# Row maximum on one core: three split rows, and 55 blocks through GpSimd in place of 38

## The chip, the cores and the metric

The kernel runs on 1 core of one Trainium2 chip. The metric is the device time of one execution in microseconds (us). The core's engines appear in the profile as PE (TensorE matmuls), PEld (its weight loads), DVE (VectorE), ACT (ScalarE), POOL (GpSimd) and SP (SyncE, which here only issues loads). Sixteen DMA engines move the data.

## What is computed

```python
def setup_inputs():
    batch, seq, dim = 32, 512, 1024
    return {"x": np.random.randn(batch, seq, dim).astype(np.float32)}

def reference(x):
    return np.max(x, axis=-1).astype(np.float32)
```

The input is 16,384 rows of 1,024 float32, 67.11 MB; the output is one float32 for each row.

## The kernel before

**Layout.** The rows are dealt to 128 partitions, so each partition gets 128 rows. From here on a "row" means one row in each partition: 128 x 1,024 float32, or 4 KB on each partition and 524,288 bytes in all. The work is 128 such rows. `BLOCKS` cuts them into loads: the first list is one contiguous block of the input of 112 rows in each partition, the second the last 16. Each number is one DMA of so many rows, called L0, L1 and so on, here L0 to L17. The last two rows are no loads: `PIECES` cuts each into two column pieces (604 + 420 and 568 + 456), each with its own DMA.

**Ring.** The loads go into one SBUF tile `ring` of `RING` = 47 rows, used again from the start once the end is reached. Its first 128 columns are `res`, where the maxima collect. `issue()` puts the loads into SP's queue in their order (line 209), each as soon as no step that still reads its part of the ring is left before it in the plan; the pieces follow (line 214). The loads' waits are on the readers of the ring's part, and on earlier loads.

**Plan.** `PLAN` is an order written out by hand for all compute engines. `in_turn` keeps each engine's instructions in that order. Its steps:

- `d<j>`: DVE takes the maximum along the columns of load j's rows, into `res` (line 74 by way of `maximum`). Rows that are shared (below) are left out.
- `SHARED = {j: (m, parts)}` says that of load j's last m rows the first `parts` blocks of 128 columns go through GpSimd. `p<j>` is DVE's maximum over the other columns of these rows, written to a small PSUM tile `got`. With `parts` = 8 there is nothing left and no `p`.
- `t<k>`: for one chunk of such blocks (at most 8 blocks) PE transposes each 128 x 128 block into PSUM (line 138), ACT copies the chunk to SBUF (line 144), and POOL takes the maximum over the partitions with a partition all-reduce (line 146).
- `b<k>`: PE brings each block's 128 maxima back to one column of `got` (line 156).
- `m<j>`: DVE takes the maximum over `got`'s partial results of load j, into `res`.
- `f<k>`: DVE takes the maximum of piece k. A row's first piece writes its maximum into the ring column just ahead of the second piece, and the second piece's instruction reads that column too.

The order of the tail before is

```python
... d16 m12 p17 t6 f0 b5 f1 f2 b6 m14 f3 m17
```

**Stores.** Both stores are issued by ACT, after all of ACT's copies. The first (the 112 columns of the first block, 56 KB, line 236) waits for `behind`, which is `f0`; the second (the last 16 columns, 8 KB, line 238) waits for the last maxima.

**Buffers.** The tiles of the GpSimd path rotate: two PSUM tiles for the transposes, two SBUF tiles for the copies, two for the all-reduce's results, and four small PSUM tiles `got`. PE has one order for transposes and returns, so a `b` that waits for POOL holds the transposes after it.

Of the kernel before, what the change touches and what calls it, by code (L numbers as in the profile page):

```python
# [10 lines left out]


BLOCKS = [
    [2, 13, 13, 15, 14, 11, 11, 10, 8, 8, 7],
    [4, 3, 2, 2, 1, 1, 1],
]
RING = 47  # L17


SHARED = {10: (3, 6), 12: (2, 6), 14: (1, 6), 17: (1, 2)}  # L20

PIECES = [(604, 420), (568, 456)]

PLAN = """
    d0 d1 d2 d3 d4 d5 d6 d7 d8 d9 t0 d10 t1 t2 p10 d11 b0 b1 t3 d12 t4 p12 d13 b2 m10 t5 d14
    p14 d15 b3 b4 d16 m12 p17 t6 f0 b5 f1 f2 b6 m14 f3 m17  # L30
""".split()

NOSYNC = mybir.DependencyInfo(mybir.DependencyClass.NoSync, mybir.DependencyReason.DATA)
# [4 lines left out]
def kernel(  # L38
# [53 lines left out]
    views = []  # L92
    last = len(PIECES)
    first = at = 0
# [13 lines left out]
    assert first == I  # L108
    shared = [SHARED.get(j, (0, C)) for j in range(len(loads))]

# [68 lines left out]
    room = I + at * D  # L179
    for q in range(len(PIECES[0])):  # L180
        for r, widths in enumerate(PIECES):
            c, w = sum(widths[:q]), widths[q]
# [85 lines left out]
```

## Time and profile before

| what | value |
|---|---|
| median of 4 runs | 163.61 us (163.54 to 163.71) |
| the profiled execution's own time | 163.55 us |
| its span | 161.8 us, of 306 instructions |
| DVE busy | 135.5 us (84%), 37 instructions |
| POOL busy | 16.2 us, 7 of its 11 instructions all-reduces |
| PE busy | 13.5 us, 76 matmuls |
| DMA | 67.18 MB, mean 415 GB/s over the span |

Between the span and the execution's time lie 1.75 us outside the profile's instructions. A busy time is an average over the span; the DVE, for example, is idle in the first quarter while the first loads arrive and has no gap of note at the end. So the order of the prediction's views goes from the whole to the last twenty microseconds.

### The profile page before, as it was taken

To read this page: it belongs to the slowest core of one execution; us is meant where nothing else is said; L and a number is where in the kernel's file an instruction comes from. 1 tells how busy PE (TensorE), PEld (TensorE's weight loads), DVE (VectorE), ACT (ScalarE), POOL (GpSimd) and SP (SyncE) were. 2 spreads that over 40 slices of the span, in tenths; PEclk is the share of its full clock that TensorE was granted. 3 is DMA by queue.
4 is the path that set the end of the run, shared out by engine and by line. 5 is a ranking of instruction groups with operands and counts; after the bars stand their busy time and mean duration, and the time that the engine had idled before them with its cause. 6 is when DMAs were issued, how large, how long until landed. Compare 5 with 4: busy or idle time off the path is not lost.

```text
span 161.8 us, 306 instructions
## 1 busy us (share of the span) xinstructions
PE 13.5 (8%) x76; PEld 11.7 (7%) x76; DVE 135.5 (84%) x37; ACT 6.5 (4%) x8; POOL 16.2 (10%) x11
## 2 busy tenths in 40 slices
PE   0000000000000000000000000000000000737662
PEld 0000000000000000000000000000000000727441
DVE  3500089969995499989999999999999999999994
ACT  3000000000000000000000000000000000231220
POOL 0000000000000000000000000000000000197991
PEclk9999999999999999999999999999999999995555
DMA  5999999995999978999898999799999999999991
GB/s 196 484 421 421 421 421 500 487 504 258 486 486 486 440 326 369 454 405 535 357 535 357 501 390 486 324 486 389 446 462 389 446 397 454 409 425 413 409 392 42
DMA packets 3456, 67.18 MB, mean 415 GB/s; under 512 B 640, under 2 KB 896, under 8 KB 1536
## 3 DMA queue, kind: packets, MB, share of 16 engines
q1 hardware_dynamic: 3168, 67.11, 97.0%
q10 hardware_dynamic: 288, 0.07, 0.2%
HBM read 67.11 MB, written 0.07 MB: 415 GB/s over the span
## 4 chain that ended last, share of the span: by engine, by line
DVE 49%; DMA 46%; another core or an unknown queue 3%; SPq 1%; issue 0%; DVEq 0%
DVE ring L74 47%; DMA ring<-in_x_dram 46%; DVE got L74 1%; SPq L209 1%; DVEq L263 0%
## 5 line engine op out<-in xcount | busy, mean ns | idle before, releaser
L74 DVE TENSOR_REDUCE ring<-ring 128x1 f32<-128x1024 f32 (+12 forms) x21 | 131.5, 6294 | 23.0 <-DMA ring<-in_x_dram 22.9
L146 POOL PARTITION_ALL_REDUCE top<-sb x7 | 16.0, 2353 | 142.0 <-ACT sb L144 142.0
L138 PE MATMUL ps<-ident,ring 128*128 128x128 f32 x38 | 8.8, 413 | 140.8 <-DMA ring<-in_x_dram 140.5
L138 PEld LDWEIGHTS ps<-ident,ring 128*128 128x128 f32 x38 | 7.4, 220 | 140.9 <-issue 140.9
L144 ACT COPY sb<-ps 128x768 f32<-128x768 f32 (+1 forms) x7 | 5.2, 739 | 150.0 <-PE ps L138 148.7
L156 PE MATMUL got<-ident,top 1*128 1x1 f32 x38 | 4.9, 237 | 4.6 <-POOL top L146 2.9
L156 PEld LDWEIGHTS got<-ident,top 1*128 1x128 f32 x38 | 4.3, 200 | 6.1 <-POOL top L146 5.4
L74 DVE TENSOR_REDUCE got<-ring 128x3 f32<-128x768 f32 (+3 forms) x4 | 3.0, 754 | 0.0
L144 ACT ACT_TABLE_LOAD x1 | 1.3, 1283 | 0.7 <-PEq L252 0.7
L79 DVE MEMSET ident<- 128x128 f32 x1 | 0.2, 165 | 0.8 <-PEq L252 0.8
L74 DVE TENSOR_REDUCE ring<-got 128x3 f32<-128x21 f32 (+3 forms) x4 | 0.6, 160 | 0.0
L86 DVE TENSOR_SCALAR rowno<-rowno 32x1 f32<-32x1 f32 x3 | 0.4, 146 | 0.1
L81 DVE TENSOR_TENSOR_SCAN colno<-ident 128x128 f32<-128x128 f32 x1 | 0.4, 424 | 0.0
L88 DVE TENSOR_SCALAR ident<-colno,rowno 128x128 f32<-128x128 f32 x1 | 0.3, 285 | 0.0
L83 DVE STREAM_TRANSPOSE rowno<-colno 128x32 f32<-128x32 f32 x1 | 0.2, 213 | 0.0
L252 POOL MEMSET const-float32-0.0<- 128x1 f32 x1 | 0.1, 99 | 0.2 <-issue 0.2
L252 POOL MEMSET const-bfloat16-1.0<- 128x1 bf16 x1 | 0.1, 102 | 0.0
L252 POOL MEMSET const-uint8-127<- 128x1 uint8 x1 | 0.1, 102 | 0.0
L252 POOL MEMSET const-float32-1.0<- 128x1 f32 x1 | 0.1, 99 | 0.0
L80 DVE MEMSET rowno<- 128x32 f32 x1 | 0.1, 85 | 0.0
## 6 DMA issues: line engine op xcount, KB each, us to landing
ring<-in_x_dram SPq DMA_DIRECT2D x2, 6656.0 KB, 27.5
ring<-in_x_dram SPq DMA_DIRECT2D x2, 5632.0 KB, 30.9
ring<-in_x_dram SPq DMA_DIRECT2D x2, 4096.0 KB, 32.3
ring<-in_x_dram SPq DMA_DIRECT2D x1, 7680.0 KB, 52.8
ring<-in_x_dram SPq DMA_DIRECT2D x1, 7168.0 KB, 36.8
ring<-in_x_dram SPq DMA_DIRECT2D x1, 5120.0 KB, 39.1
ring<-in_x_dram SPq DMA_DIRECT2D x1, 3584.0 KB, 39.4
ring<-in_x_dram SPq DMA_DIRECT2D x3, 1024.0 KB, 38.2
```

The costliest lines, as they stand in the source:

```text
L74: return in_turn("DVE", nc.vector.reduce_max(out=out, in_=in_, axis=X))
L79: in_turn("DVE", nc.vector.memset(ident, 1.0))
L81: in_turn("DVE", nc.vector.tensor_tensor_scan(out=colno, data0=ident, data1=ident, initial=-1.0, op0=ALU.add, op1=ALU.mult))
L83: in_turn("DVE", nc.vector.transpose(out=rowno, in_=colno[:, :32]))
L86: in_turn("DVE", nc.vector.tensor_scalar(out=part, in0=part, scalar1=float(q * 32), scalar2=None, op0=ALU.add))
L88: identity = in_turn("DVE", nc.vector.tensor_scalar(out=ident, in0=colno, scalar1=rowno[:, 0:1], scalar2=None, op0=ALU.is_equal))
L138: in_turn("PE", nc.tensor.transpose(out=ps[:, w:w + P], in_=rows(j)[:, loads[j][1] - m + r + i, c * P:(c + 1) * P], identity=ident,))
L144: in_turn("ACT", nc.scalar.copy(out=sb[:, :W], in_=ps[:, :W]))
L146: in_turn("POOL", nc.gpsimd.partition_all_reduce(top[:, :W], sb[:, :W], P, bass_isa.ReduceOp.max))
L156: in_turn("PE", nc.tensor.transpose(out=share(j)[:, c, r + i:r + i + 1], in_=tops[k][0:1, w:w + P], identity=ident[0:1, 0:1],))
L209: load = nc.sync.dma_start(out=rows(issued), in_=src)
L252: nc = _bacc.Bacc("TRN2", target_bir_lowering=False, num_devices=1)
```

## The change

The loads become fewer and larger at the start (up to 16 rows), three rows in place of two are cut in two pieces, with the first pieces of the three rows loaded one after the other and then the second pieces, and eight loads in place of four give blocks to GpSimd: 55 blocks in ten chunks in place of 38 in seven. The first of them comes early (one row of L3, two blocks). The DVE gets 7 partials in place of 4 and 8 merges in place of 4. Loads and pieces together are 22 DMAs in both.

```diff
 BLOCKS = [
-    [2, 13, 13, 15, 14, 11, 11, 10, 8, 8, 7],
-    [4, 3, 2, 2, 1, 1, 1],
+    [2, 13, 16, 16, 15, 13, 12, 10, 9, 6],
+    [4, 3, 2, 2, 1, 1],
 ]
 RING = 47
-SHARED = {10: (3, 6), 12: (2, 6), 14: (1, 6), 17: (1, 2)}
+SHARED = {3: (1, 2), 7: (1, 3), 8: (2, 8), 9: (6, 2), 10: (4, 2), 11: (1, 6), 13: (2, 2), 15: (1, 4)}
-PIECES = [(604, 420), (568, 456)]
+PIECES = [(488, 536), (560, 464), (624, 400)]
 PLAN = """
-    d0 d1 d2 d3 d4 d5 d6 d7 d8 d9 t0 d10 t1 t2 p10 d11 b0 b1 t3 d12 t4 p12 d13 b2 m10 t5 d14
-    p14 d15 b3 b4 d16 m12 p17 t6 f0 b5 f1 f2 b6 m14 f3 m17
+    d0 d1 d2 d3 t0 p3 b0 m3 d4 d5 d6 t1 d7 p7 t2 d8 t3 b1 b2 t4 m7 p9 t5 b3 t6 m8 p10 b4 b5
+    d11 t7 p11 m9 d12 b6 m10 p13 t8 b7 d14 t9 m11 p15 f0 b8 f1 m13 f2 f3 f4 b9 f5 m15
 """.split()
```

## The prediction

> **What bounds the kernel now.** I read the page first, then the table of windows, the waits of SP's queue, the timeline of the tail, and the groups by shape.
>
> ```profile
> span 161.8 us, 306 instructions
> ...
> PE 13.5 (8%) x76; PEld 11.7 (7%) x76; DVE 135.5 (84%) x37; ACT 6.5 (4%) x8; POOL 16.2 (10%) x11
> ...
> q1 hardware_dynamic: 3168, 67.11, 97.0%
> ```
>
> The DVE is the busiest engine, yet the load queue q1 occupies the DMA engines for 97.0% of the span. The windows say where (columns: span, length, PE, PEld, DVE, ACT and POOL busy, PE clock, DMA share, GB/s):
>
> ```profile
> 71.80:110.60 38.80, 0.00 (x0) 0.00 (x0) 38.67 (x3) 0.00 (x0) 0.00 (x0) 1.00 0.99 427
> 154.00:155.00 1.00, 0.57 (x6) 0.49 (x6) 1.00 (x2) 0.67 (x1) 1.00 (x2) 0.50 1.04 418
> 156.50:157.00 0.50, 0.22 (x2) 0.00 (x0) 0.50 (x2) 0.18 (x1) 0.50 (x1) 0.50 1.04 376
> 158.20:158.40 0.20, 0.01 (x1) 0.00 (x0) 0.20 (x2) 0.00 (x0) 0.20 (x1) 0.50 0.00 0
> 158.40:158.60 0.20, 0.14 (x2) 0.14 (x2) 0.20 (x1) 0.00 (x0) 0.01 (x1) 0.50 0.11 31
> 158.60:158.80 0.20, 0.20 (x2) 0.15 (x2) 0.20 (x3) 0.00 (x0) 0.00 (x0) 0.50 0.84 235
> 158.80:159.00 0.20, 0.03 (x1) 0.00 (x0) 0.20 (x3) 0.00 (x0) 0.00 (x0) 0.50 0.09 20
> ```
>
> The DMA share stays near 1 until the last piece, so no ring wait starves the queue; the little traffic from 158.4 on is the first store, alone. Both DMA and DVE are full from 71.8 on.
>
> ```profile
> SPq L214 <- DMA ring<-in_x_dram: 18.2, 4, 8.1
> ```
>
> Each of the four pieces was issued when the load eight places ahead landed: L10 to L13 at 138.56, 143.47, 147.16, 149.64 (112, 116, 119, 121 rows). Issue plus time to landing gives the others: L2 36.74 (28 rows), L4 71.86 (57), L5 85.12 (68), L7 110.61 (89), L9 130.05 (105), and the last piece 149.64 + 9.0 = **158.64**. L2 to L10 is 84 rows and 8 DMAs in 101.82 us: with 0.05 for a DMA, **1.2075 us a row**. The last 16 rows and 11 DMAs took 20.08 us, which leaves **0.07 for a small DMA**.
>
> ```profile
> 71.86 71.22 DVE L74 TENSOR_REDUCE ring<-ring 128x14 f32<-128x14336 f32 x7 [0.78 <-DMA ring<-in_x_dram]
> ...
> 157.67 0.38 ACTq L236 DMA_DIRECT2D out_dram<-ring  x1
> ...
> 158.80 0.62 DVE L74 TENSOR_REDUCE ring<-ring 128x1 f32<-128x457 f32 x1
> 159.33 0.15 DVE L74 TENSOR_REDUCE ring<-got 128x1 f32<-128x3 f32 x1
> 159.52 0.34 ACTq L238 DMA_DIRECT2D out_dram<-ring  x1
> ```
>
> The last reduction starts 0.16 after its piece lands, held by f2 and m14; m17 ends at **159.48** and the last store follows. So the end is set by two chains that are level: the last landing plus one small reduction, and the DVE's backlog.
>
> ```profile
> L74 DVE TENSOR_REDUCE ring<-ring 128x8 f32<-128x8192 f32 x2 | 17.4, 8683 | 0.0
> L74 DVE TENSOR_REDUCE ring<-ring 128x1 f32<-128x1024 f32 x4 | 4.8, 1211 | 0.0
> ...
> L74 DVE TENSOR_REDUCE ring<-got 128x1 f32<-128x7 f32 x1 | 0.2, 155 | 0.0
> ```
>
> From 8 rows (8.683) and one (1.211) a DVE row costs 1.0674 us and an instruction 0.14 on top; each starts 0.08 before the one ahead ends (d10 at 138.67, d9 ended 138.75), so 0.06 net for a reduction and 0.075 for a merge. Test on before: from d7's start, 110.64, 49 rows less 38 blocks (4.75 rows) are 44.25 rows, 47.23 us; 18 reductions 1.08, 4 merges 0.30, the last overlap 0.08: 159.33. Measured 159.48: **0.15 of small waits** to carry over.
>
> **The change part by part.**
>
> *Loads.* Both versions have 128 rows and 22 DMAs, so by the row law the last landing stays at 158.64 if the queue is never empty. Ring waits: L4 waits for d1 (35.07, as before), L5 for d2 (57.6), L6 for d3, p3 and t0 (76.8), L7 for d4 (94.0), L8 and L9 for d5 (108), the rest for d6 (121) or for the load eight places ahead. At each of these at least one load of 12 rows or more (14 us) is still to land. On SP, whatever waits holds what is behind it, and there are always those 14 us. Cost 0; were that cover gone, a stall would go straight to the end.
>
> *Pieces.* One row more goes in pieces, one one-row load and one large load fewer. At equal DMA count that is 0. By the windows, pieces move at 376 GB/s and one-row loads at 418: 1.394 against 1.254 us a row, +0.14. The row law meets the four pieces' own landings (156.76, 157.57, 158.06, 158.64) within 0.1, so I take 0.05, nearer to 0. A rule speaks against this part. "DMA: Bandwidth & Descriptors" (the Trainium skill, section on the anatomy of one DMA) fits 2.0 us plus bytes over 436 GB/s to each GpSimd-issued DMA; by that, six pieces against four would be an estimated 4 us more if each were paid in turn. The row above it says otherwise for queued ones: the 228 KB piece landed 0.58 us after the 210 KB one.
>
> *The DVE's backlog.* L6 of after is 87 rows in 7 DMAs: 110.61 - 2 x 1.2075 - 0.05 = 108.14. d4 starts at L4's landing (62 rows: 77.9), ends 94.0, d5 at 107.9, so the DVE waits 0.2 for L6. The early p3, t0, b0 and m3 (0.94 + 0.15 on the DVE) lie before L4's landing (d3 from 59.7 to 75.9) and cost nothing; without that gap 1.1. From 108.17: 53 rows less 53 blocks (6.625) are 46.375 rows, 49.50 us; 18 reductions 1.08; 7 merges 0.53; overlap 0.08: 159.36, with the 0.15 of waits **159.51**. Seventeen blocks taken from the DVE are 2.27 us, but 15 of them only pay for the later start: fewer rows are done by L6 (87, where L7 had 89) and three merges and two partials more lie in the tail. The backlog stays level.
>
> *GpSimd's path.* 768 columns take 2.5 to 2.58 us and 256 took 1.1 (3.63 for the last two), so 1,024 take 3.27, 512 take 1.82. Two transposes took 0.66 and six 1.51, eight are 1.94; copies 0.80 and 0.37, so 1.01; six returns 0.80, so eight 1.02. L8 (106 rows) lands at 131.2: t2 and t3 hold POOL from 134.3 to 140.9; L9 at 138.5: t4 from 141.6, t5, then t6 to 150.0; b6 ends 151.1, and the DVE wants m10 at 108.17 + 40.375 rows and 12 instructions = 152.0. t9: L15 lands at 154.60; transposes 1.09, copy 0.59, all-reduce 1.82, returns 0.59 and 0.25 of handoffs end at 158.95, with m15 wanted at 159.3. Hidden, by 0.9 and 0.4 us. A 1,024-wide one is not in the trace: from 2.6 (the 768 row) to 4.4 (four times the 256 row); 3.27 lies on the line through both rows.
>
> *The first store.* It waits for f0 (ends 156.2) and is behind ACT's t9 copy (156.4); before it was issued at 157.67, 0.8 before its traffic, which then met no load. Now that traffic falls at 157.2 to 157.6, among the last pieces. Price: 0.2 x (0.11 + 0.84 + 0.09) = 0.21 us of all 16 engines; bounds 0 and 0.21 on the last landing. As the share there is 1.03 and nothing is free, I take 0.21. The same page's section on issuing engines says that DMAs from different engines share the 16 and interleave; by it 0.21, were queues separate 0.
>
> *Sum.* Last landing 158.64 + 0.05 + 0.21 = 158.90; f5 (401 columns, 0.56) starts at 158.93, m15 0.08 before its end, 0.15 long: **159.56**. The backlog says 159.51. The later is 0.08 after 159.48; the profiled execution of 163.55 becomes 163.63, and as the median of the runs is 0.06 above it, **163.7**. The two small pieces' gain (f3's 0.62 is now 0.56, 0.1 less waiting) is eaten by the store.
>
> **The rivals.**
>
> *GpSimd late (slower).* POOL has 0.73 us idle between t3 and t4, then t4, t5, t6 run on end. If an 8-block all-reduce takes x longer than 3.27, b6 is 4x - 0.73 later; it decides from x = 0.41 (0.9 of slack). At 0.65 more (a fifth) m10 is 1.0 late and all the DVE's tail with it: 164.7. For: no 1,024-wide row. Against: 768 ran at 2.5 to 2.58 every time, DVE busy or not.
>
> *Landing sooner (faster).* Without the collision the end is 0.26 sooner by landing, but the backlog holds 159.51: no gain. Over 0.33 needs the loads faster too, say 0.05 less for each of seven large DMAs, which moves L6 and the end by 0.35: 163.3. Against: 13 rows took 15.70 and 15 rows 18.14, both 1.21 a row.
>
> *The 16-row loads aren't single runs (slower).* They put 65,536 bytes on a partition; the longest in the trace is 61,440. Cut into 4 KB runs, 32 rows at 1.254 in place of 1.2075 lose 1.5 us: 165.2. Nothing in the trace hints at it.
>
> **How the numbers follow.** No change that can be told, as summed: 0.74, its own range 163.4 to 164.0. GpSimd late 0.12, landing sooner 0.08, runs cut 0.04, the rest 0.02. A measurement of this kernel tells about 0.2% (0.33 us) from no change. Of the forecast's 0.74, some 0.08 lies above that (piece bound of 0.14, the 0.15 of waits doubled, m15 late) and 0.01 below. Faster 0.09, same 0.65, slower 0.26. The range reaches to 164.4, into the late GpSimd, and down to 163.35.
>
> **What would show it.** Right: last piece landing at 158.6 to 159.0, the first store at about 156.4, no DVE wait after 108.2 over 0.3, L6 at 108.1, all-reduces of 1,024 at 3.3, 3,168 packets on q1. Wrong: a DVE wait on a return, PE's or POOL's; DMA share under 0.95 in a window between 40 and 157 us; a landing 0.4 or more from 158.9.

## The result and the profile after

The changed kernel takes **163.73 us** (median of 53 runs, 163.52 to 165.51), the kernel before 163.62 us (73 runs, 163.51 to 164.07). Their ratio is 1.003, with a 95% interval of 1.0019 to 1.0041. Median and ratio differ because the 53 times lie in two groups: 37 from 163.52 to 164.08 (median 163.66) and 16 from 164.93 to 165.51 (median 165.18). Nothing lies between, and no time of the kernel before lies in the upper group. So seven executions in ten are level with before, as forecast, and three in ten take some 1.5 us more. I call the second kind "late"; what makes them late is the subject of the experiments. Their spans, from 163.1 to 163.7 us against 161.7 to 162.2, hold all of it.

The profiled execution is one of the level ones, 163.56 us. Its page (row 5 has busy time, mean ns and idle time before):

```profile
span 161.8 us, 399 instructions
PE 20.6 (13%) x110; PEld 17.2 (11%) x110; DVE 133.6 (83%) x41; ACT 8.6 (5%) x11; POOL 23.4 (14%) x14
...
q1 hardware_dynamic: 3168, 67.11, 96.9%
q10 hardware_dynamic: 288, 0.07, 0.2%
q8 instruction: 1, 0.02, 0.0%
...
L146 POOL PARTITION_ALL_REDUCE top<-sb x10 | 23.2, 2356 | 134.9 <-ACT sb L144 134.9
```

The span is that of before to 0.1 us. The DVE has 1.9 us less to do and POOL 7.2 us more, off the path. One line is new: queue q8, of the kind that the profile calls instruction, moved one packet of 16,384 bytes. I read it as a fetch of a part of an engine's program (e2 shows that it is PE's); PE's instructions rose from 76 to 110 pairs of a weight load and a matmul.

The timeline of the tail, beside the lines shown of before:

```profile
77.35 0.16 DVE L74 TENSOR_REDUCE ring<-got 128x1 f32<-128x3 f32 x1 [0.53 <-PE got L156]
...
108.22 22.61 DVE L74 TENSOR_REDUCE ring<-ring 128x12 f32<-128x12288 f32 x2 [0.19 <-DMA ring<-in_x_dram]
...
156.28 0.38 ACTq L236 DMA_DIRECT2D out_dram<-ring  x1
...
156.95 2.49 DVE L74 TENSOR_REDUCE ring<-ring 128x1 f32<-128x624 f32 x4
...
159.36 0.15 DVE L74 TENSOR_REDUCE ring<-got 128x1 f32<-128x5 f32 x1
...
159.54 0.34 ACTq L238 DMA_DIRECT2D out_dram<-ring  x1
```

L6's reduction starts at 108.22 after a wait of 0.19. From there the DVE waits neither for a load nor for a return: m15 ends at 159.51, against m17's 159.48. The one wait on a return is m3's, at 77.35, for b0; the DVE waits 0.45 us more for L4 right after it, so it costs nothing. The DMA view of this tail (KB, us from issue to landing) has the second thing that is new:

```profile
out_dram<-ring ACTq DMA_DIRECT2D x1, 56.0 KB, 4.0
out_dram<-ring ACTq DMA_DIRECT2D x1, 8.0 KB, 1.4
```

The first store needed 4.0 us to land, where it had needed 1.6. It was issued at 156.28, but its first packet went at 157.88, when the loads were nearly drained (their last packet ends at 158.24). 135 of its packets have gone by 158.5. The other nine, the share of one of 16 DMA engines (144 / 16), go from 159.17 to 159.58. The trace does not name a packet's engine, but the fetch runs from 158.11 to 159.19, so I read it as one engine held by the fetch. As the last store is issued only at 159.54, this delay costs nothing here.

### The profile page after: what moved, and what is told of

Same layout as the page of the kernel before. It is cut to its first block, busy times and chain, and to the rows that moved or that the text cites. A ratio compares the mean times of both kernels' runs of the same rounds, so it can differ in the third digit from the quotient of the medians.

```text
span 161.8 us, 399 instructions
## 1 busy us (share of the span) xinstructions
PE 20.6 (13%) x110; PEld 17.2 (11%) x110; DVE 133.6 (83%) x41; ACT 8.6 (5%) x11; POOL 23.4 (14%) x14
## 2 busy tenths in 40 slices
DMA packets 3457, 67.19 MB, mean 415 GB/s; under 512 B 640, under 2 KB 1024, under 8 KB 1664
## 3 DMA queue, kind: packets, MB, share of 16 engines
q1 hardware_dynamic: 3168, 67.11, 96.9%
## 4 chain that ended last, share of the span: by engine, by line
DVE 47%; DMA 44%; issue 5%; another core or an unknown queue 1%; SPq 0%; DVEq 0%
DMA ring<-in_x_dram 44%; DVE ring L74 41%; DVE got L74 7%; SPq L209 0%; DVEq L263 0%
## 5 line engine op out<-in xcount | busy, mean ns | idle before, releaser
L74 DVE TENSOR_REDUCE ring<-ring 128x2 f32<-128x2048 f32 (+13 forms) x18 | 119.5, 6666 | 24.4 <-DMA ring<-in_x_dram 24.4
L146 POOL PARTITION_ALL_REDUCE top<-sb x10 | 23.2, 2356 | 134.9 <-ACT sb L144 134.9
L138 PE MATMUL ps<-ident,ring 128*128 128x128 f32 x55 | 13.7, 426 | 116.1 <-DMA ring<-in_x_dram 106.1
L138 PEld LDWEIGHTS ps<-ident,ring 128*128 128x128 f32 x55 | 10.6, 223 | 116.7 <-issue 115.8
L144 ACT COPY sb<-ps 128x1024 f32<-128x1024 f32 (+4 forms) x10 | 7.4, 747 | 147.2 <-PE ps L138 147.2
L74 DVE TENSOR_REDUCE got<-ring 128x1 f32<-128x768 f32 (+6 forms) x7 | 12.9, 1845 | 0.0
L156 PE MATMUL got<-ident,top 1*128 1x1 f32 x55 | 7.4, 244 | 22.4 <-DVE got L74 16.4
L156 PEld LDWEIGHTS got<-ident,top 1*128 1x128 f32 x55 | 6.6, 212 | 25.1 <-issue 17.8
L74 DVE TENSOR_REDUCE ring<-got 128x1 f32<-128x3 f32 (+7 forms) x8 | 1.3, 157 | 0.5 <-PE got L156 0.5
```

The costliest lines, as they stand in the source:

```text
L74: return in_turn("DVE", nc.vector.reduce_max(out=out, in_=in_, axis=X))
L138: in_turn("PE", nc.tensor.transpose(out=ps[:, w:w + P], in_=rows(j)[:, loads[j][1] - m + r + i, c * P:(c + 1) * P], identity=ident,))
L144: in_turn("ACT", nc.scalar.copy(out=sb[:, :W], in_=ps[:, :W]))
L146: in_turn("POOL", nc.gpsimd.partition_all_reduce(top[:, :W], sb[:, :W], P, bass_isa.ReduceOp.max))
L156: in_turn("PE", nc.tensor.transpose(out=share(j)[:, c, r + i:r + i + 1], in_=tops[k][0:1, w:w + P], identity=ident[0:1, 0:1],))
```

## The experiments

Late executions here are those above 164.5 us. "PE" is the number of PE's instructions that the trace records, waits included; a transpose is two of them. Nearly all late executions have spans of 162.9 us or more. Two have not, counted in brackets: one of e1 (164.95) and one of e11 (164.89) have spans of 162.1 and 162.0, like the level ones beside them, and what they take longer lies outside the profile's instructions. Whatever delayed these two did not delay the last store.

| kernel | PE | q8 packet in the profile, us | late | median us (before beside it) | ratio, 95% interval |
|---|---|---|---|---|---|
| before | 167 | none | 0 of 73 | 163.62 | |
| after | 242 | 158.11 | 16 of 53 | 163.73 (163.62) | 1.0019 to 1.0041 |
| e1, 50 blocks | 218 | 158.36 | 2 of 12 (+1) | 163.86 (163.64) | 1.001 to 1.0053 |
| e2, before + 40 | 247 | 158.02 | 1 of 11 | 163.69 (163.64) | 0.9993 to 1.0027 |
| e3, after + 12 | 266 | 158.13 | 6 of 12 | 164.20 (163.64) | 1.0013 to 1.0059 |
| e4, store late | 242 | 158.39 | 3 of 12 | 163.75 (163.64) | 1.0004 to 1.0051 |
| e5, fewer returns | 168 | none | 0 of 11 | 164.08 (163.84) | 1.0004 to 1.0022 |
| e9, after + 80 | 402 | 142.34 | 5 of 5 | 165.07 (163.83) | 1.0068 to 1.0094 |
| e10, before + 12 | 191 | none | 0 of 11 | 163.78 (163.83) | 0.9993 to 1.001 |
| e11, before + 24 | 215 | none | 0 of 12 (+1) | 164.00 (163.83) | 1.0006 to 1.0024 |

The kernel before was some 0.2 us slower beside e5 to e11 than beside e1 to e4, so each is read against the before of its own row.

**e1: the two early shares left out.**

```diff
-SHARED = {3: (1, 2), 7: (1, 3), 8: (2, 8), 9: (6, 2), 10: (4, 2), 11: (1, 6), 13: (2, 2), 15: (1, 4)}
+SHARED = {8: (2, 8), 9: (6, 2), 10: (4, 2), 11: (1, 6), 13: (2, 2), 15: (1, 4)}
-    d0 d1 d2 d3 t0 p3 b0 m3 d4 d5 d6 t1 d7 p7 t2 d8 ...
+    d0 d1 d2 d3 d4 d5 d6 d7 t0 d8 ...
```

> The changed kernel without the shares of L3 and L7: 50 blocks in place of 55, 20 PE instructions and their waits fewer (222 recorded or less in place of 242), two partials and two merges fewer on the DVE. Of 53 executions of the changed kernel 37 took 163.5 to 164.1 us and 16 took 164.9 to 165.5. Theory A, a fetch of instructions: its trace has one packet of 16 KB on the instruction queue q8, at 158.2 to 159.2, which the kernel before has not; PE's longer program calls for it, and where it gets in ahead of the last loads' packets the end is 1.4 us later. Then here q8 is gone and no execution lies above 164.5; the times are 163.6 to 164.0, as the DVE has 0.25 us more to do after L6. Theory B, the earlier first store among the pieces: the store still falls at 156.3, so about three in ten stay near 165.2. Theory C, the 65,536-byte runs of L2 and L3: they are still there, so three in ten stay near 165.2.

Nine times lie at 163.71 to 164.01 (median 163.84) and three at 164.95 to 165.55. The packet is still there, at 158.36: 218 instructions are still too many. The step meant to remove the fetch did not remove it, so this run decides nothing between the theories. The level times are some 0.2 us above the changed kernel's 163.66, about what was expected of the DVE, but half of that lies outside the span (1.91 us between span and time, 1.80 in the changed kernel).

**e2: the kernel before with a longer PE program.**

```diff
+    ps = psum.tile([P, D], F32)
+    for _ in range(40):
+        in_turn("PE", nc.tensor.transpose(out=ps[:, :P], in_=ident, identity=ident))
```

> The kernel before with 40 transposes of the identity more at its start (between 2.5 and 12 us, PE has nothing else to do there; their result is not used): 80 PE instructions more, 247 recorded in place of 167. Loads, stores, DVE and GpSimd work are those of before. Theory A: one 16 KB packet on q8 near the end, and a part of the executions, a tenth to all, at 164.8 to 165.6 us. Theories B and C: 163.6 us throughout, as before.

The packet appears, at 158.02, in a kernel whose loads, stores and plan are those of before. One of eleven executions is late, at 165.33, with a span of 163.5. That PE's longer program calls the fetch is shown; that it makes executions late is only hinted at by one of eleven.

**e3: the changed kernel with 12 such transposes (the same edit in after, `range(12)`).**

> The changed kernel with 12 transposes of the identity at its start: 24 PE instructions more, so that the instruction at which the fetch is asked for is reached some 3 to 4 us sooner, with loads still queued. Theory A: the 16 KB packet falls at about 154 to 156, always ahead of the last pieces, and all or nearly all executions are at 164.3 to 165.5. Theories B and C: as the changed kernel, seven in ten at 163.7, three in ten at 165.2.

Six of twelve are at 164.72 to 165.16, the others at 163.55 to 163.68. More are late, but not nearly all; and in the profile, a level one, the packet still lies at 158.13. The fetch had not moved ahead of the last pieces, so theory A in this form misses.

**e4: the first store held until f4.**

```diff
-            if behind is None:
+            if k == 4:
                 behind = inst
```

> The changed kernel with its first store held until f4 (158.9) in place of f0. Theory B: no execution above 164.5. Theories A and C: three in ten stay near 165.2 us. Beside that, by the prediction's term for the store, the last landing comes up to 0.21 us sooner and the executions not delayed take 163.55 in place of 163.65.

Three of twelve stay late (165.03 to 165.40), so the early store is not the cause. The other nine have a median of 163.71, not the 163.55 that the prediction's store term asks for, against 163.66 of the changed kernel: holding the store back gains nothing. By the prediction's sums it could gain little in any case, as the DVE's backlog holds the end at 159.51.

**e5: one return for each row of a chunk, in place of one for each block.** The kernel leaves out the other blocks' maxima, so its output is not the rows' maximum, and its merges read fewer values; the rest is kept.

```diff
 def back(k):
...
-            for c in range(parts):
+            for c in range(1):
...
 def merge(j):
...
+        some = share(j)[:, 0:parts + 1:parts, :] if parts < C else share(j)[:, 0:1, :]
```

> The changed kernel with one return of a block for each row of a chunk in place of one for each block (18 returns in place of 55); the other blocks' results are left out, and a merge reads only what was written. 74 PE instructions fewer: 168 recorded, about the 167 of the kernel before. Loads with their 65,536-byte runs, the early first store, POOL's and ACT's work, the DVE's partials and every wait of a merge on a return stay. Theory A (a longer PE program brings a 16 KB instruction fetch, which in some executions delays the last loads): no packet on q8, no execution above 164.5, the times at 163.55 to 163.95. If the long runs of L2 and L3, the store or the all-reduces were behind the late executions: three in ten near 165.2 us.

Eleven times, all between 163.99 and 164.16, beside a before of 163.75 to 164.01. All lie above the 163.55 to 163.95 that I expected. The spans do not (161.9 to 162.1, as before's); the extra lies outside them, 2.06 us in place of before's 1.78, and is not explained. The DMA view has no q8 any more:

```profile
DMA packets 3456, 67.18 MB, mean 415 GB/s; under 512 B 640, under 2 KB 1024, under 8 KB 1664
...
q1 hardware_dynamic: 3168, 67.11, 96.9%
q10 hardware_dynamic: 288, 0.07, 0.2%
```

The 65,536-byte loads, the early store, the ten all-reduces and the order of the merges are all still there. Were three in ten late as in the changed kernel, none of eleven would have a chance of 0.7 to the 11th, 2%. Taking PE instructions away took the fetch and the late executions away together.

**e6 to e8: profiles of three single executions.** e6 and e7 run e3's kernel, e8 the changed one.

> The changed kernel with 12 transposes of the identity at its start once more, for one profile. Half of its executions took 164.7 to 165.2. In one of these, theory A: the 16 KB packet starts before 157, with loads still queued, the last landing is 1 to 1.4 us later than 158.7 and f5 waits for it. Rival A2: the fetch falls after the loads as before, and PE waits for its instructions: b9 comes late and m15 waits for it, with the landings unchanged. In the other half: the packet at 158.1 to 158.4.

> The same kernel, one more profile, with the same two readings: an execution above 164.5 us shows a 16 KB packet before 157 and late landings (A), or unchanged landings and a late b9 (A2).

> The changed kernel itself, one more profile, with the same two readings: above 164.5 us the 16 KB packet lies before 157 and the landings behind it are late (A), or the landings are unchanged and b9 is late (A2); at 163.5 to 164.1 us the packet lies at 158.1 to 158.4.

e6 caught a late execution: 164.94 us. e7 (163.83) and e8 (163.72) are level, with the packet at 158.19 and 158.24, as expected of a level one. For the late one both readings that I had written down are wrong. e6's tail in the timeline:

```profile
159.07 0.56 DVE L74 TENSOR_REDUCE ring<-ring 128x1 f32<-128x401 f32 x1
159.55 0.15 DVE L74 TENSOR_REDUCE ring<-got 128x1 f32<-128x5 f32 x1
159.73 0.34 ACTq L242 DMA_DIRECT2D out_dram<-ring  x1
```

Loads, PE and DVE end on time: m15 at 159.70, the last store issued at 159.73. What is late comes after that. The same execution's DMA view from 159.5 to 163 us, then SP's waits:

```profile
q10 hardware_dynamic: 144, 0.01, 2.7%
q8 instruction: 1, 0.02, 1.7%
issues: line engine op xcount, KB each, median us to landing
out_dram<-ring ACTq DMA_DIRECT2D x1, 8.0 KB, 2.6
```

```profile
SPq L267 <- DMA out_dram<-ring: 4.3, 2, 3.0
```

and the same two lines in e7:

```profile
out_dram<-ring ACTq DMA_DIRECT2D x1, 8.0 KB, 1.4
...
SPq L267 <- DMA out_dram<-ring: 3.1, 2, 2.5
```

The fetch runs here from 160.32 to 161.29, and the last store lands 2.6 us after its issue in place of 1.4. 135 of its 144 packets start from 160.57 on within 0.3 us; the last nine, again one engine's share, start from 161.28 on, as the fetch ends. SP's wait for the stores, 3.1 us in e7, is 4.3 here: **the 1.2 us by which the execution is late**. Its span is 163.2, e7's 162.0. Half of the 1.2 us is the late packets themselves: the last one ends at 161.35, in e7 at 160.75. The other half lies between the last packet and the landing, 0.98 us in place of 0.36, and what fills it the trace does not show. Reading A2, that the end waits for PE's instructions, does not fit: PE's last matmuls are done by 159.3, before the fetch starts, and PE's next recorded instruction comes 0.30 us after the store's landing in e6 as in e7.

So, by this reading, the fetch holds one of 16 DMA engines for 1 us. At 158.1 it meets the first store, which has time; at 160.3 it meets the last store, for which the end waits.

**e9: the changed kernel with 80 transposes more.**

> The changed kernel with 80 transposes of the identity at its start (160 PE instructions more, 402 recorded). Theory A3, after the look at a late execution: the 16 KB instruction fetch holds up the packets of a store on its one DMA engine; at 158.2 it meets the first store and costs nothing, at 160.4 it meets the last store, whose nine packets on that engine then come 1 us late and move the end by 1.2 to 1.5. If the place in PE's program where the fetch is asked for sets its time, it is asked for here some 20 us sooner, is served at the latest when the loads end at 158.2, and no execution lies above 164.5 us: 163.55 to 163.85 throughout. If the fetch's time does not depend on PE's place, or more than one fetch comes, three to five in ten stay near 165.

All five times are 165.06 to 165.27, the opposite of what I expected. The fetch did move with PE's place in its program, to 142.34, but it didn't wait for the loads' end. The DVE's timeline:

```profile
144.98 3.36 DVE L74 TENSOR_REDUCE got<-ring 128x4 f32<-128x3072 f32 x1 [0.69 <-DMA ring<-in_x_dram]
148.67 2.29 DVE L74 TENSOR_REDUCE ring<-ring 128x2 f32<-128x2048 f32 x1 [0.33 <-DMA ring<-in_x_dram]
...
160.85 0.15 DVE L74 TENSOR_REDUCE ring<-got 128x1 f32<-128x5 f32 x1
```

L10 lands at 144.97 where it landed at 143.46 in after; p10 waits 0.69 us and d11 0.33, and m15 starts 1.49 us later than after's 159.36. Some 0.2 us of both was there before the fetch (L9 landed at 138.76, in after at 138.57), so the fetch's part is 1.3. This is theory A as first stated: among the loads, the fetch delays one engine's share of all that follows, and the end with it. The last load packets show it too: from 158.64 they start one at a time, mostly some 0.07 us apart, until 159.75, as one engine's would that is a microsecond behind the others. So the fetch cost 1.2 to 1.3 us in the two places where a profile shows its cost, over the last store (e6) and among the loads (e9), and nothing between the last load and the last store.

**e10 and e11: where the fetch begins (e2's edit with `range(12)` and `range(24)`).**

> The kernel before with 12 transposes of the identity at its start: 191 PE instructions recorded, between 168 (no fetch) and 218 (a fetch). One or the other: no packet on q8 and all times at 163.5 to 163.95, or one packet and about a tenth to three tenths of the executions near 165.2.

> The kernel before with 24 such transposes: 215 PE instructions recorded. By A3 one packet of 16 KB on q8, as at 218, and some executions near 165.2 us; without a packet, none above 164.5.

Neither profile has the packet, at 191 and 215 recorded instructions; e1 has it at 218. I had expected it at 215. e10 is level throughout (one time, 164.11, is above the range given). e11 has one time of 164.89 beside eleven of 163.86 to 164.06. Its span of 162.0 is theirs, so it is not late in the way of e6 or e9. The eleven lie 0.15 us above before, outside the span, like e5's, and this is open too.

## Why the prediction was right or wrong

The number and the range held: 163.7 was forecast for 163.73, in 163.35 to 164.4, and the likeliest case, that the two level chains stay level, is what 37 of 53 executions show. By the median the change is +0.07%, inside the 0.2% that I called no change; by the ratio, +0.3%, it is slower, because the mean carries the late executions. That part was forecast by no case. The close hit of 163.7 is partly luck: the level executions have a median of 163.66, and the late ones lift it to 163.73.

- **Row law and ring waits.** L4 landed at 77.9, L6 at 108.2, L8 at 131.3 (77.9, 108.1, 131.2 forecast); 3,168 packets. The DMA share was 0.95 to 1.06 in the stages from 36.7 to 158.1 us, so no ring wait starved the queue (windows of 4 us between 40 and 64 us scatter in both kernels, from 0.71 to 1.13 in before and from 0.72 to 1.21 in after, so a low one is no sign of a stall). The 16-row loads ran at the row law, so that rival is out.
- **DVE's backlog.** It began at 108.22 and reached m10 at 152.06 (152.0 forecast) and m15's end at 159.51 (159.51 by the backlog). Right to the size of its parts. As the DVE never waited after 108.22, it was this chain that set the end, and not the last landing, which the sum had put later (159.56).
- **GpSimd's times.** The 1,024-wide all-reduce took 3.26 us (3.27), the 512-wide 1.78 (1.82); b9 ended at 159.09 and m15 started at 159.36. Hidden, so the rival of a late GpSimd is out.
- **Pieces.** From L8's landing to the last one, 22 rows and 13 DMAs took 158.80 - 131.26 = 27.54 us; the row law gives 22 x 1.2075 + 13 x 0.07 = 27.48. The term of 0.05 stands at 0.06.
- **The first store, a mis-sized term.** It was priced at 0.21 us on the last landing, with its traffic 0.8 after the issue. Its packets came from 1.60 after the issue on, when all but 50 of the 3,168 load packets had started, and the row law leaves 0.01 for it. The term measured about 0. e4, without the store there, is no faster, but could have shown little of it. The last landing came at 158.80 in place of 158.90, and 0.07 of its difference from before's 158.64 was there at the first load already (the DVE's first reduction started at 5.37, not 5.30). The forecast of 0.08 over before was right partly by luck: this term stood where other small differences were.
- **The step that failed: GpSimd's path costed by its engines' time alone.** Each added block is a transpose and a return, four PE instructions; 17 blocks are 68. They were priced at nothing because PE is idle, and in time that is right. What they bring is a 16 KB fetch, which no row of before could show because it didn't happen there, and with it, as e5 and e6 indicate, the 16 of 53 executions that take 1.5 us more. "Runtime: NRT & Kernel Launch" of the Trainium skill (section on instruction fetch mechanics) says that a program is fetched in 16 KiB blocks of 256 instructions, and that the cost of crossing from one to the next is mostly hidden. The size is that of the packet; hidden it was, if all late executions are the fetch's, in 37 of 53.

What stays open is why the same program's fetch falls at 158.1 in some executions and at 160.3 in others (seen in e3's kernel). In the seven level profiles that have it, it starts 0.04 to 0.28 us before the end of the last load packet, whether the trace records 218 PE instructions or 266; that looks like a wait for the loads, but e9's fetch, in the midst of the loads, does not fit it. By the profiles the threshold lies between 215 (e11) and 218 recorded instructions (e1), in two different programs; what sets it is not shown. I saw one late execution's profile with the fetch near the end, of e3's kernel, and none of the changed kernel's. That its 16 late ones have the same cause is inferred from e5 and from their longer spans. Their size does not settle it: they are 1.5 us above its level ones, where e3's are 1.25 above theirs and the fetch cost 1.2 in e6 and 1.3 in e9.

## What to carry to other kernels

An instruction on an idle engine is not always free, as it makes that engine's program longer: look in the DMA queues of the page for an instruction line, and count instructions for each engine before and after. Where the loads fill the DMA engines and the end waits for a store, one extra packet of 1 us on one of the 16 engines can move the end by that much and more (1.2 and 1.3 us here). Look at all times of a kernel before reading its median: two groups ask for a profile of each.

## What the runs showed that I had not expected

- A 16,384-byte instruction fetch took 0.97 to 1.11 us in the nine profiles that have it. It delayed the last store by 1.2 us (e6), the loads behind it by about 1.3 us (e9), and the first store, without cost, by 1.3 us in after (4.0 us to land, 2.7 in e5 and e6).
- A store issued by ACT while the load queue was full began late: its first packet came 1.60 us after the issue in after, with 50 load packets still to start, and 0.88 in before, where the loads had ended. In e9, where one engine lagged, the store's first packets went at 158.68 and its last nine only from 159.76 on, behind the 17 load packets that started in between.
- PE's granted clock in the profile's tail was 0.50 in before and 1.00 in after. Eight transposes took 1.94 us in after, at 1.00, as the prediction had worked out from rows at 0.50, and 1.94 in e4, at 0.50: in these rows the clock made no difference.
